# Gate and up products of a convolutional FFN by Strassen's rule, over two token halves, with the down product as a stage of its own

## The chip, the cores and the metric

The kernel runs on one core of a Trainium2 chip. The metric is the time of one execution on the device, in microseconds; of several runs the median. TensorE does the matrix products (PE in the profile; PEld is its loading of weights), VectorE (DVE) and ScalarE (ACT) and GpSimd (POOL) the element-wise work. Only VectorE and ScalarE read TensorE's results, which lie in eight PSUM banks of 512 fp32 columns; GpSimd works on SBUF alone. SyncE's queue (SP) issues loads, ScalarE's queue some stores.

## What is computed

One layer of a decoder for 1024 prompt tokens and 8 x 4 sample tokens, 1056 columns in all, in fp32: a combined projection, two token mixers, an output projection, and an FFN with a causal convolution of width 3 on the gate rows. The change touches what comes after the mixers:

```python
mix = jax.nn.sigmoid(gate_a) * y_a + jax.nn.sigmoid(gate_b) * y_b    # y_a, y_b: branch products
x = x + (mix @ w_out).astype(dt)                                     # w_out [1024, 1024]

h2 = _rmsnorm(x, g_ffn)
gc, new_ffn = _causal_conv(h2 @ w_ffn_gate, ffn_buf, w_ffn_conv)     # w_ffn_gate, w_ffn_up [1024, 2816]
x = x + ((jax.nn.silu(gc) * (h2 @ w_ffn_up)) @ w_ffn_down).astype(dt)  # w_ffn_down [2816, 1024]
# after the layer: y = _rmsnorm(x, g_final)
```

## The kernel before

Every operand of a large product is held as two rounded parts, hi and lo (`split`, line 82: a cast on ScalarE, line 83, and a subtraction on VectorE, line 84), and a product is three matmuls for each block of 128 input rows: hi x hi, hi x lo, lo x hi (`mm3`, lines 106 to 111). Activations lie in [channel, token] layout, eight blocks of 128 channels by 1056 tokens. `load_w` (line 86) fetches 256 weight columns in two loads of 512 KB on SP's queue and splits them; `proj_cm` (line 125) multiplies 128 of those columns with three blocks of 352 tokens, each in a PSUM bank of the pool `psd`, which has four.

After the mixers come the branch products (lines 1160 to 1179), blocks of 352 tokens; the output projection (lines 1195 to 1215), 256 columns at a time over nine token tiles, with residual, second norm (`norm`) and transposition to [channel, token] (`to_cm`); then the FFN. The 2816 features are 22 tiles of 128, taken two at a time in 11 chunks. `gate_up` does for each tile of a chunk three blocks for the gate, the convolution (`conv_proj`, one multiplication, line 229, and two fused steps, line 231, on VectorE; SiLU on ScalarE, line 232), then three blocks for up, each multiplied with the gate (line 1266) and split into `act` (lines 1268 and 1269). `down` (line 1276) multiplies the chunk's two tiles with 2 x 1024 down weights and adds the results to the residual `x1` in SBUF (line 1289; the sample rows line 1293). The loop emits `gate_up(ch + 1)` ahead of `down(ch)`, so that gate, up and down products alternate for the whole FFN, and `act` has two places. The last chunk's `down` ends each token tile with the final norm and its store.

The order in each engine's queue is not written by hand: the framework places an instruction when its inputs and buffers are ready, and prefers what stands earlier in the program.

Of the kernel before, what the change touches and what calls it, by code (L numbers as in the profile page):

```python
# [16 lines left out]
P = 128  # L17
# [16 lines left out]
OFF_Q, OFF_K, OFF_V, OFF_AB, OFF_OGA = 0, 512, 1024, 1536, 1544  # L34
OFF_QB, OFF_FB, OFF_IB, OFF_OGB, OFF_GA, OFF_GB = 2056, 2568, 3080, 3592, 4104, 5128
# [7 lines left out]
def hybrid_step(ctx: ExitStack, tc: tile.TileContext, ins, outs):  # L43
# [23 lines left out]
    # ---------------------------------------------------------------- constants  # L67
# [10 lines left out]
    # ---------------------------------------------------------------- helpers  # L78
# [6 lines left out]

    def load_w(parts, eng=None):
        """parts: list of halves; a half is a list of (row chunk count, DRAM AP [rows, 128 columns])."""
        hi = wpool.tile([P, KD, 256], F32R, name="whi")
        lo = wpool.tile([P, KD, 256], F32R, name="wlo")
        for j, half in enumerate(parts):  # L90
            raw = wpool.tile([P, KD, P], F32, name="wraw")
# [23 lines left out]
    def mm_s(ps, st, whi, wlo, ks):  # L115
        """The sample tokens' rows: st holds (hi | lo) columns; rows NS.. of ps take the low part's share."""
# [8 lines left out]
    def proj_cm(W, j, m, evac, src=None):  # L125
        """Generator: one block of BW tokens per step."""
# [10 lines left out]
    class Fill:  # L137
        """Dense work that is emitted between the steps of a token mixer."""
# [30 lines left out]
    def norm(t, xt, g_bc, work, xn, sq=None):  # L169
        """RMSNorm of token tile t (rows of xt), scaled by g_bc, into xn."""  # L170
# [8 lines left out]
    def to_cm(t, xn, dst):  # L179
        """Token tile t to [channel, token] layout, split into dst."""  # L180
# [14 lines left out]
    # ---------------------------------------------------------------- DRAM scratch  # L195
# [9 lines left out]
    def conv_proj(W, j, width, wT, cacheT, out_cache, dst, dst_s, zp, src=None):  # L205
        """Generator: project 128 channels, causal conv along tokens, SiLU; dst [P, SEQ], dst_s [P, NBAT * STEP]."""
# [26 lines left out]
        # the outputs of batch b start at column pad + SEQ + b * per of co  # L233
# [17 lines left out]
    # ---------------------------------------------------------------- first norm, first projections  # L251
    cwT = const.tile([P, 12, 28], F32, name="cwT")
    fwT = const.tile([P, NFF, 19], F32, name="fwT")
    lbT = const.tile([P, H, 2], F32, name="lbT")
    cout = const.tile([P, 12, 27], F32, name="cout")
    qkv_s = const.tile([P, 3, H, 32], F32, name="qkv_s")     # the sample tokens' columns stay on chip
# [14 lines left out]
    wab = ini.tile([P, KD, 16], F32R, name="wab")     # (hi | lo) of the decay and beta columns  # L271
# [95 lines left out]
    ab = const.tile([P, NT, 8], F32, name="ab")  # L367
# [12 lines left out]
    # ---------------------------------------------------------------- masks  # L380
    ones = const.tile([P, P], F32, name="ones")
    nc.gpsimd.memset(ones, 1.0)
    eem = const.tile([P, 2, P], F32, name="eem")      # (j<i | j<=i), rows j, columns i
# [4 lines left out]
    slow = const.tile([P, P], F32, name="slow")       # m > j  # L388
# [4 lines left out]
    bm = const.tile([P, NBLK, STEP], F32, name="bm")      # row and column belong to the same block  # L393
# [5 lines left out]
    m96 = const.tile([96, NBAT], F32, name="m96")         # a head's tokens and batches, three times  # L399
    for i in range(3):  # L400
        nc.gpsimd.tensor_copy(m96[32 * i:32 * i + 32, :], bm[32 * i:32 * i + 32, NBAT * i:NBAT * (i + 1), 0])
    eem_s = const.tile([P, 2, P], F32, name="eem_s")
    for k in range(2):
        nc.gpsimd.tensor_tensor(eem_s[:, k, :], eem[:, k, :], bmf, ALU.mult)
    slow_s = const.tile([P, P], F32, name="slow_s")
    nc.gpsimd.tensor_tensor(slow_s, slow, bmf, ALU.mult)
    last_s = const.tile([P, NBLK, STEP], F32, name="last_s")
# [931 lines left out]
```

## Time and profile before

| | |
|---|---|
| median of 3 runs | 1815.76 us (1807.79 to 1821.93) |
| span of the profiled execution | 1813.2 us |
| TensorE busy in it | 1766.7 us, 97% |
| VectorE / ScalarE / GpSimd busy | 52% / 28% / 10% |
| moved by DMA | 161.67 MB, mean 89 GB/s |
| branch products, out projection, FFN | from about 830, 930, 1035 us |

The times of instructions come from the profiled execution, which is one of its own; its span stands 2.6 us under the median of the runs. Matmuls overlap: a matmul's own duration is longer than the distance to the next, so the distance from start to start says what one costs.

### The profile page before, as it was taken

The page shows a single profiled execution, that of the slowest core. Times are in us where ns is not written, and L with a number is a line of the kernel's source. Part 1 is how long each engine was busy: PE and PEld are TensorE (multiplying, and loading weights), DVE is VectorE, ACT ScalarE, POOL GpSimd, SP SyncE. Part 2 cuts the span into 40 slices and gives each one's busy share as a digit, 9 for nine tenths or more (in the row PEclk, how much of TensorE's full clock was granted, in tenths as well). Part 3 has the DMA queues.
Part 4 walks back from the last instruction along what each step waited for, and adds up shares of the span by engine and source line. Part 5 has one row for each costly group of instructions (what it writes and reads, how often), then busy time and mean ns, then how long its engine had stood idle before and what let it go on. Part 6 is the DMA issues. An engine that isn't in the chain of part 4 may idle for free.

```text
span 1813.2 us, 28073 instructions
## 1 busy us (share of the span) xinstructions
PE 1766.7 (97%) x11591; PEld 1678.6 (93%) x11591; DVE 935.9 (52%) x1634; ACT 516.4 (28%) x1133; POOL 179.7 (10%) x332
## 2 busy tenths in 40 slices
PE   6999999999999999999999999999999999999998
PEld 6999898989899999999999999989989899899896
DVE  5555555756464657415542644453453454544456
ACT  5432525343332223323110432112112112122122
POOL 2200101111010234200000100000000000000001
PEclk9999999999998989999999999999999999999999
DMA  5233343453333434463433111111111111111102
GB/s 163 82 116 105 108 134 106 134 169 108 100 91 100 136 106 143 119 220 99 140 120 89 50 48 44 36 46 47 47 47 47 47 47 47 47 47 47 47 27 109
DMA packets 199947, 161.67 MB, mean 89 GB/s; under 512 B 17982, under 2 KB 186064, under 8 KB 199801
## 3 DMA queue, kind: packets, MB, share of 16 engines
q1 hardware_dynamic: 175382, 123.92, 23.5%
q10 hardware_dynamic: 24438, 35.96, 5.5%
q8 instruction: 91, 1.49, 0.3%
q14 instruction: 36, 0.29, 0.0%
HBM read 119.57 MB, written 40.21 MB: 88 GB/s over the span
## 4 chain that ended last, share of the span: by engine, by line
PE 78%; DVE 10%; DMA 3%; ACT 3%; issue 3%; POOL 1%; SPq 1%; ACTq 0%; POOLq 0%; DVEq 0%
PE pd L109 22%; PE pd L110 22%; PE pd L111 22%; DVE Pt L745 3%; PE pm L974 2%; DVE X L747 2%; DVE wlo L84 1%; DMA Db<-dU 1%; PE pd L121 1%; POOL rs L76 1%; DMA Yd<-dX 1%; DVE y L177 1%; POOL pss L76 1%; PE pm L606 0%; PE pm L829 0%
## 5 line engine op out<-in xcount | busy, mean ns | idle before, releaser
L109 PE MATMUL pd<-hhi,whi 128*128 128x352 f32 x1056 | 348.3, 330 | 0.4 <-ACT z L218 0.4
L111 PE MATMUL pd<-hhi,wlo 128*128 128x352 f32 x1056 | 346.3, 328 | 0.0
L110 PE MATMUL pd<-hlo,whi 128*128 128x352 f32 x1056 | 346.0, 328 | 0.0
L109 PE MATMUL pd<-mhi,whi 128*128 128x352 f32 x1056 | 340.5, 323 | 0.0
L110 PE MATMUL pd<-mlo,whi 128*128 128x352 f32 x1056 | 338.6, 321 | 0.7 <-DVE mlo L84 0.7
L111 PE MATMUL pd<-mhi,wlo 128*128 128x352 f32 x1056 | 338.3, 321 | 0.0
L84 DVE TENSOR_TENSOR wlo<-wraw,whi 128x1024 fp32r<-128x1024 f32 x130 | 157.6, 1223 | 204.7 <-ACT whi L83 204.2
L83 ACT CAST whi<-wraw 128x1024 fp32r<-128x1024 f32 x130 | 135.2, 1051 | 407.6 <-PE pd L111 202.0
L109 PEld LDWEIGHTS pd<-hhi,whi 128*128 128x128 f32 x1056 | 200.4, 190 | 1.9 <-ACT z L218 0.6
L110 PEld LDWEIGHTS pd<-hlo,whi 128*128 128x128 f32 x1056 | 200.7, 190 | 1.1 <-DVE hlo L84 0.4
L111 PEld LDWEIGHTS pd<-hhi,wlo 128*128 128x128 f32 x1056 | 200.3, 190 | 0.6
L110 PEld LDWEIGHTS pd<-mlo,whi 128*128 128x128 f32 x1056 | 198.4, 188 | 1.3 <-DVE mlo L84 0.9
L109 PEld LDWEIGHTS pd<-mhi,whi 128*128 128x128 f32 x1056 | 198.0, 188 | 0.4
L111 PEld LDWEIGHTS pd<-mhi,wlo 128*128 128x128 f32 x1056 | 198.0, 188 | 0.0
L1289 DVE TENSOR_TENSOR x<-x,pd 128x512 f32<-128x512 f32 x176 | 118.9, 686 | 78.0 <-PE pd L111 77.7
L109 PE MATMUL pd<-whi,act 128*128 128x512 f32 x352 | 138.0, 392 | 0.1
L110 PE MATMUL pd<-wlo,act 128*128 128x512 f32 x352 | 137.2, 390 | 0.0
L111 PE MATMUL pd<-whi,act 128*128 128x512 f32 x352 | 137.0, 389 | 0.0
L1266 DVE TENSOR_TENSOR ga<-pd,ga 128x352 f32<-128x352 f32 x66 | 34.5, 523 | 98.5 <-PE pd L111 98.5
L218 ACT COPY z<-pd 128x352 f32<-128x352 f32 (+1 forms) x102 | 44.1, 442 | 137.4 <-PE pd L111 129.4
L109 PEld LDWEIGHTS pd<-whi,act 128*128 128x128 f32 x352 | 66.1, 188 | 16.2 <-PE pd L111 2.0
L111 PEld LDWEIGHTS pd<-whi,act 128*128 128x128 f32 x352 | 66.1, 188 | 14.1
(411 smaller groups left out, 2760.5 us busy)
## 6 DMA issues: line engine op xcount, KB each, us to landing
wraw<-in_w_in SPq DMA_DIRECT2D x48, 512.0 KB
wraw<-in_w_ffn_gate SPq DMA_DIRECT2D x22, 512.0 KB
wraw<-in_w_ffn_up SPq DMA_DIRECT2D x22, 512.0 KB
wraw<-in_w_ffn_down SPq DMA_DIRECT2D x22, 512.0 KB
sg_d<-sg ACTq DMA_DIRECT2D x16, 528.0 KB
qkv_d<-sl ACTq DMA_DIRECT2D x12, 512.0 KB
sgb<-sg_d SPq DMA_DIRECT2D x12, 352.0 KB
sga<-sg_d SPq DMA_DIRECT2D x12, 352.0 KB
```

Source lines behind the costliest of these rows:

```text
L76: nc.gpsimd.tensor_tensor(out, in_, pexp[:n, which, :w], ALU.pow)
L83: nc.scalar.copy(out=hi, in_=src)
L84: (eng or nc.vector).tensor_tensor(lo, src, hi.bitcast(F32), ALU.subtract)
L109: nc.tensor.matmul(ps, whi[:, kw], xhi[:, kx], start=q == 0, stop=False)
L110: nc.tensor.matmul(ps, whi[:, kw], xlo[:, kx], start=False, stop=False)
L111: nc.tensor.matmul(ps, wlo[:, kw], xhi[:, kx], start=False, stop=q == n - 1)
L218: nc.scalar.copy(out=z[:, pad + a:pad + e], in_=ps[:, :e - a])
L745: nc.vector.tensor_tensor(Pt[:, :, 0:w], X[:, :, 0:w], Db[:, 0:w, r:w].rearrange("p s o -> p o s").broadcast_to([P, 8, w]), ALU.mult)
L747: nc.vector.tensor_reduce(X[:, :, r], Pt[:, :, 0:w], axis=mybir.AxisListType.X, op=ALU.add)
L974: nc.tensor.matmul(ps[:, cc * 64:(cc + 1) * 64].rearrange("p (n r) -> p n r", r=s), kk[:, cs], rhs, start=True, stop=True)
L1266: nc.vector.tensor_tensor(a[:, bs], ps, a[:, bs], ALU.mult)
L1289: nc.vector.tensor_tensor(x1[:, t, qs], x1[:, t, qs], ps, ALU.add)
```

## The change

Gate and up products: for two feature tiles and two token groups of equal width n (256 in the first half of the tokens, 272 in the second, which holds the sample tokens) the eight products of half the input channels become seven, by the Strassen-Winograd rule. `wino` computes them into four PSUM banks, three of which are used twice; ScalarE, VectorE and GpSimd combine them into the four blocks of the result. The weights' combinations are formed by GpSimd (`wino_weights`, once for each half), the activations' by VectorE and GpSimd (`wino_acts`, once for each half). The second half's operands are laid where the first half's lie. Weight buffers are a pool of five (`w8`) and four raw ones.

The result of the FFN's first part goes to DRAM (`act_d`), the residual too (`x1_d`). After all 44 calls the down product runs as a stage of its own: `load_act` fetches and splits a chunk's input, ahead of `down` of the chunk before; the first chunk writes its sums by ScalarE, the later ones add on VectorE; GpSimd adds the residual. The branch products go over four token blocks of 256 and 272 in place of three of 352. Constants of the mixers are freed after them.

```diff
-    for nb in range(NB):
+    for i, (b0, b1) in enumerate(QT):        # (0,256) (256,512) (512,784) (784,1056)
...
+    def wino_weights(w, f0):
+        r0, r1 = wraw(), wraw()
+        for r, f in ((r0, f0), (r1, f0 + 1)):
+            nc.sync.dma_start(out=r, in_=w[:, f * P:(f + 1) * P].rearrange("(k p) n -> p k n", p=P))
...
+        def group(src, n):
+            t = w8("wg").rearrange("p a b -> p (a b)").rearrange("p (s k n) -> p s k n", s=2, n=P)
+            split(t[:, 0, :n], t[:, 1, :n], src)
+            out.append(t)
+        a11, a12, a21, a22 = r0[:, :HK], r0[:, HK:], r1[:, :HK], r1[:, HK:]
...
+        yield out
+        s12 = pair_tile("s12")
+        nc.gpsimd.tensor_tensor(s12[:, HK:], a21, a22, ALU.add)
+        nc.gpsimd.tensor_tensor(s12[:, :HK], s12[:, HK:], a11, ALU.subtract)
+        group(r0, KD)
+        yield
+        s34 = pair_tile("s34")
+        nc.gpsimd.tensor_tensor(s34[:, :HK], a11, a21, ALU.subtract)
+        nc.gpsimd.tensor_tensor(s34[:, HK:], a12, s12[:, :HK], ALU.subtract)
+        group(s12, KD)
+        yield
+        group(s34, KD)
+        yield
+        group(a22, HK)
+        yield
...
+    def wino(W, X, n, gt, steps, c11, c12, c21, c22):
+        banks = [PSD(f"x{i}") for i in range(4)]
+        x1, x6, x5, x7 = (b[:, :n] for b in banks)
...
+            for k in range(HK):
+                w = W[g][:, :, k0 + k]
+                nc.tensor.matmul(ps, w[:, 0], hi[:, k], start=start and k == 0, stop=False, skip_group_check=True)
+                nc.tensor.matmul(ps, w[:, 0], lo[:, k], start=False, stop=False, skip_group_check=True)
+                nc.tensor.matmul(ps, w[:, 1], hi[:, k], start=False, stop=k == HK - 1, skip_group_check=True)
...
+        mm(0, x1, True)
+        m1 = tmp("m1")
+        nc.scalar.copy(out=m1, in_=x1)
+        mm(1, x6, True)
+        u2 = tmp("u2")
+        nc.vector.tensor_tensor(u2, m1, x6, ALU.add)
+        next(steps, None)
+        mm(2, x5, True)
+        m5 = tmp("m5")
+        nc.scalar.copy(out=m5, in_=x5)
+        mm(3, x7, True)
+        u3 = tmp("u3")
+        nc.vector.tensor_tensor(u3, u2, x7, ALU.add)
+        c22(u3, m5)
+        mm(4, x1, False)
+        c11(x1)
+        next(steps, None)
+        mm(5, x5, False)
+        c12(u2, x5)
+        next(steps, None)
+        mm(6, x7, False)
+        c21(u2, x7)
+        next(steps, None)
...
+    def wino_acts(src, n, tb, ops):
...
+        split(*ops[0], b11)
+        nc.vector.tensor_tensor(t1, b12, b11, ALU.subtract)
+        nc.vector.tensor_tensor(t2, b22, t1, ALU.subtract)
+        yield
+        split(*ops[1], t2)
+        nc.gpsimd.tensor_tensor(b12, b22, b12, ALU.subtract)
+        yield
+        split(*ops[2], t1)
+        nc.gpsimd.tensor_tensor(t4, b21, t2, ALU.subtract)
...
+    def gate(f0, half, X, W, steps, ga, z):
...
+        wino(W, X, n, gt, steps,
+             lambda x: nc.scalar.copy(out=z[:, 0, 2:2 + n], in_=x),
+             lambda u, x: q2(0, lambda o, c, t: nc.vector.tensor_tensor(o, cut(u, c, t), cut(x, c, t), ALU.add)),
+             lambda u, x: nc.vector.tensor_tensor(z[:, 1, 2:2 + n], u, x, ALU.add),
+             lambda u, m: q2(1, lambda o, c, t: nc.gpsimd.tensor_tensor(o, cut(u, c, t), cut(m, c, t), ALU.add)))
...
+            nc.scalar.activation(co[:, f, :cw], z[:, f, 0:cw], AF.Copy, scale=wT[:, 0:1])
+            for q in (1, 2):
+                nc.vector.scalar_tensor_tensor(co[:, f, :cw], z[:, f, q:q + cw], wT[:, q:q + 1], co[:, f, :cw],
+                                               ALU.mult, ALU.add)
+        nc.scalar.activation(ga[:, :, :MID], co[:, :, :MID], AF.Silu)
...
+    def up(f0, half, X, W, steps, ga, a):
...
+             lambda u, m: nc.gpsimd.tensor_tensor(a[:, 1, n:w], u, m, ALU.add))
+        nc.vector.tensor_tensor(a[:, 0, n:w], a[:, 0, n:w], ga[:, 0, n:w], ALU.mult)
+        nc.vector.tensor_tensor(a[:, 1, :w], a[:, 1, :w], ga[:, 1, :w], ALU.mult)
+        nc.scalar.dma_start(out=act_d[f0:f0 + 2, :, t0:t0 + w].rearrange("f p t -> p f t"), in_=a[:, :, :w])
+    todo = [(half, f0, k) for half in range(2) for f0 in range(0, NFF, 2) for k in range(2)]
...
+    def load_act(ch):
         s0 = 2 * (ch % 2)
...
+        r = fp.tile([P, 2, T], F32, name="ra")
+        nc.sync.dma_start(out=r, in_=act_d[2 * ch:2 * ch + 2].rearrange("f p t -> p f t"))
+        nc.scalar.copy(out=ahi[:, s0:s0 + 2, :T], in_=r)
+        hv = ahi[:, s0:s0 + 2].bitcast(F32)
+        nc.vector.tensor_tensor(alo[:, s0:s0 + 2, :SEQ], r[:, :, :SEQ], hv[:, :, :SEQ], ALU.subtract)
+        nc.vector.tensor_tensor(ahi[:, s0:s0 + 2, T:], r[:, :, SEQ:], hv[:, :, SEQ:T], ALU.subtract)
...
+    nc.sync.dma_start(out=x1s, in_=x1_d[SEQ:, :])
+    x1r = post.tile([P, KD, 2 * 2 * QW], F32, name="x1r", tag="mA")
+    nc.sync.dma_start(out=x1r[:, :, :D], in_=x1_d[:SEQ, :].rearrange("(t p) d -> p t d", p=P))
...
+    Wd = load_down(0)
+    load_act(0)
     for ch in range(NCH):
         if ch + 1 < NCH:
-            gate_up(ch + 1)
+            Wn = load_down(2 * ch + 2)
+            load_act(ch + 1)
...
+        down(ch, *Wd)
+        Wd = Wn
```

## Rows read from the trace of the kernel before

**Rows 1.** The page's head: span, busy time and share of each engine, granted clock.

```profile
span 1813.2 us, 28073 instructions
PE 1766.7 (97%) x11591; PEld 1678.6 (93%) x11591; DVE 935.9 (52%) x1634; ACT 516.4 (28%) x1133; POOL 179.7 (10%) x332
...
PEclk9999999999998989999999999999999999999999
```

**Rows 2.** Table by stage: stretch, length, busy time of each engine (instructions), clock, DMA, GB/s.

```profile
830.00:932.00 102.00, 99.57 (x624) 98.90 (x624) 66.14 (x99) 28.64 (x41) 0.00 (x0) 0.98 0.46 134
...
1029.00:1050.00 21.00, 18.74 (x127) 17.80 (x126) 13.85 (x22) 10.55 (x22) 3.23 (x7) 1.00 0.18 51
1050.00:1758.00 708.00, 707.88 (x4040) 662.70 (x4039) 329.70 (x459) 148.22 (x261) 27.59 (x85) 1.00 0.15 45
```

**Rows 3.** Timeline of TensorE, gate and up: start, duration in us; first and last of 26.

```profile
1299.72 0.32 PE L110 MATMUL pd<-mlo,whi 128*128 128x352 f32 x1
...
1303.68 0.32 PE L111 MATMUL pd<-mhi,wlo 128*128 128x352 f32 x1
```

**Rows 4.** The same in the output projection: first and last of 21.

```profile
984.58 0.28 PE L111 MATMUL pd<-whi,mlo 128*128 128x256 f32 x1
...
986.96 0.28 PE L110 MATMUL pd<-wlo,mhi 128*128 128x256 f32 x1
```

**Rows 5.** The same in the down product: first and last of 10.

```profile
1769.78 0.39 PE L110 MATMUL pd<-wlo,act 128*128 128x512 f32 x1
...
1771.82 0.39 PE L110 MATMUL pd<-wlo,act 128*128 128x512 f32 x1
```

**Rows 6.** Groups of VectorE by shape: count, busy us, mean ns, idle time before and releaser.

```profile
L84 DVE TENSOR_TENSOR wlo<-wraw,whi 128x1024 fp32r<-128x1024 f32 x130 | 157.6, 1223 | 204.7 <-ACT whi L83 204.2
L1289 DVE TENSOR_TENSOR x<-x,pd 128x512 f32<-128x512 f32 x176 | 118.9, 686 | 78.0 <-PE pd L111 77.7
...
L1293 DVE TENSOR_TENSOR x1s<-x1s,pd 32x512 f32<-32x512 f32 x44 | 28.2, 672 | 1.1 <-PE pd L123 0.7
...
L1207 DVE TENSOR_TENSOR x<-res,pd 128x256 f32<-128x256 f32 x32 | 13.4, 419 | 48.3 <-PE pd L111 48.2
L720 DVE SCALAR_TENSOR_TENSOR UA<-pm,pr,EE 128x256 f32<-128x256 f32 x32 | 13.2, 474 | 0.0
...
L84 DVE TENSOR_TENSOR mlo<-pm,mhi 128x512 fp32r<-128x512 f32 x16 | 10.5, 680 | 0.0
...
L177 DVE SCALAR_TENSOR_TENSOR tmp<-x,rs,tmp 128x1024 f32<-128x1024 f32 x8 | 10.3, 1285 | 5.6 <-POOL rs L76 5.6
```

**Rows 7.** The same for ScalarE.

```profile
L83 ACT CAST whi<-wraw 128x1024 fp32r<-128x1024 f32 x130 | 135.2, 1051 | 407.6 <-PE pd L111 202.0 <-PE pd L110 133.3 <-PE pd L123 66.2
```

**Rows 8.** The same for GpSimd.

```profile
L989 POOL TENSOR_TENSOR kk<-kk,tots 128x256 f32<-128x256 f32 x48 | 35.1, 734 | 34.3 <-issue 13.2 <-PE pm L974 11.3 <-PE pm L962 4.3
...
L658 POOL TENSOR_TENSOR Sb<-Sb,eGl_s 128x512 f32<-128x512 f32 x8 | 8.3, 1040 | 73.1 <-DMA Sb<-in_state_delta 63.7 <-DMA Db<-dU 9.3
```

**Rows 9.** Line 654 (min/median/max ns), and timeline of VectorE and GpSimd at 701 us.

```profile
L654 DVE TENSOR_TENSOR um<-st,m x16: 676/679/1479, 316.6 to 738.8; 96x512 fp32r<-96x512 f32 x16
...
701.33 1.48 DVE L654 TENSOR_TENSOR um<-st,m 96x512 fp32r<-96x512 f32 x1
...
701.22 1.04 POOL L658 TENSOR_TENSOR Sb<-Sb,tots_s 128x512 f32<-128x512 f32 x1 [3.34 <-DMA Sb<-in_state_hgrn]
```

**Rows 10.** Timeline of VectorE in the FFN.

```profile
1108.88 1.32 DVE L231 SCALAR_TENSOR_TENSOR co<-z,fwT,co 128x1072 f32<-128x1072 f32 x1
1110.12 0.51 DVE L1266 TENSOR_TENSOR ga<-pd,ga 128x352 f32<-128x352 f32 x1
1110.56 1.32 DVE L231 SCALAR_TENSOR_TENSOR co<-z,fwT,co 128x1072 f32<-128x1072 f32 x1
```

**Rows 11.** Timeline of SP's queue at the largest load, and two us of it by stage.

```profile
772.52 1.52 SPq L1146 DMA_DIRECT2D raw<-oT_d  x3
...
778.00:780.00 2.00, 2.00 (x14) 2.00 (x13) 0.00 (x0) 0.00 (x0) 0.00 (x0) 1.00 1.01 408
```

**Rows 12.** Table by stage: the ten us around TensorE's gap at 830 us.

```profile
830.00:840.00 10.00, 7.92 (x39) 7.54 (x39) 7.95 (x14) 9.97 (x19) 0.00 (x0) 0.83 0.47 143
```

More of the change, by code (lines that the diff above doesn't have):

```diff
@@ new lines, in to_raw @@
+    def to_raw(t):
+        n = rows(t)
+        dst, c0 = (hA, t * P) if t * P < MID else (hB, t * P - MID)
+        for g in range(2):
+            ps = PSM()
+            pv = ps.rearrange("p (k n) -> p k n", k=4)
+            for k in range(4):
+                nc.tensor.transpose(out=pv[:, k, :n], in_=x1t(t)[:n, (4 * g + k) * P:(4 * g + k + 1) * P],
+                                    identity=ident[:n, :n])
+            nc.scalar.copy(out=dst[:, 4 * g:4 * g + 4, c0:c0 + n], in_=pv[:, :, :n])
@@ L1195, in hybrid_step, with first_weights @@
+    def first_weights():
+        g = wino_weights(wg, 0)
+        return next(g), g
     for q in range(4):
@@ L1225, in hybrid_step @@
-    last = {}
+                norm2(t)
+                if 3 <= t < 7:
+                    to_raw(t - 3)
+                if t in (4, 5):
+                    next(gen_n)
+                if t == 6:
+                    o1 = post.tile([P, 2, KD, 2 * QW], F32R, name="o1", tag="mA")
+                    o1 = o1.rearrange("p a k t -> p (a k t)").rearrange("p (i s k t) -> p i s k t", i=4, s=2, k=HK)
+                    opsA = [(o1[:, i, 0, :, :256], o1[:, i, 1, :, :256]) for i in range(4)]
+                    opsA += [None] * 3
+                    genA = wino_acts(hA, 256, hT[:, KD * MID:], opsA)
+                    for _ in range(2):
+                        next(genA)
@@ new lines, in hybrid_step, with fetch, mixed, mixedB @@
+    todo = [(half, f0, k) for half in range(2) for f0 in range(0, NFF, 2) for k in range(2)]
+    for _ in gen_n:
+        pass
+    queue = []
+    def fetch(i):
+        if i < len(todo):
+            g = wino_weights((wg, wu)[todo[i][2]], todo[i][1])
+            queue.append((next(g), g))
+    fetch(1)
+    W = Wn
+    late = []
+    for i, (half, f0, k) in enumerate(todo):
+        fetch(i + 2)
+        Wnext, gn = queue.pop(0) if queue else (None, iter(()))
+        if i == 0:
+            def mixed(gn):
+                for _ in genA:
+                    pass
+                next(gn)
+                to_raw(4)
+                yield
+                to_raw(5)
+                next(gn)
+                yield
+                to_raw(6)
+                next(gn)
+                yield
+                to_raw(7)
+                to_raw(8)
+                next(gn)
+                yield
+            gn = mixed(gn)
+        elif half == 0 and i == NCH * 2 - 1:
+            genB = wino_acts(hB, QW, hT[:, :KD * MID], opsB)
+            def mixedB(gn):
+                next(gn)
+                yield
+                next(genB)
+                next(genB)
+                next(gn)
+                yield
+                next(genB)
+                next(gn)
+                yield
+                next(genB)
+                next(gn)
+                yield
+            gn = mixedB(gn)
+        X = opsA if half == 0 else opsB
+        n2 = (i // 2) % 2
+        if k == 0:
+            gate(f0, half, X, W, gn, gab[n2], zb[n2])
+        else:
+            up(f0, half, X, W, gn, gab[n2], ab_[n2])
+        if half == 0 and i == NCH * 2 - 1:
+            for _ in genB:
+                pass
+        W = Wnext
```

298 lines of the change are left out of this document (189 added, 109 removed).

## The prediction

> **What bounds the kernel now.** I read the head of the page first: TensorE is busy for 97% of the span and holds the full clock in nearly every slice, VectorE is busy 52%, GpSimd 10% [rows 1]. A busy TensorE is not yet a saturated one, so the second view is the table by stage: from 1050 to 1758 us, where the FFN runs, TensorE has no idle time at all, VectorE is busy 47% and GpSimd 4%; in the branch and out projections before it the gaps are a few us [rows 2]. The third view is the stream of matmuls itself, for the distance from start to start. A 352-column matmul starts every 158.4 ns (25 distances from 1299.72 to 1303.68 us) [rows 3], a 256-column one every 119.0 ns (20 distances from 984.58 to 986.96) [rows 4], a 512-column one every 226.7 ns (9 from 1769.78 to 1771.82) [rows 5]. So the FFN is bound by TensorE's columns: 0.41 ns a column between 256 and 352, and some 14 ns that each matmul costs whatever its width. What the other engines do there is hidden, and may grow until it isn't.
>
> **What the change removes.** A pair of feature tiles takes 288 matmuls of 352 columns for gate and up, 11 pairs take 3168: 3168 x 0.1584 = 501.8 us. After, one call of the 7-product routine is 7 x 4 x 3 = 84 matmuls, 256 wide in the first token half and 272 in the second, and there are 22 calls for each half: 1848 x 0.1190 + 1848 x 0.1256 = 452.0 us (0.1256 by the slope above) [rows 3, 4]. That is 49.8 us less. 7/8 of the work would be 62.7 us less; the rest goes on more and narrower matmuls.
>
> **What it adds, in order of the program.**
>
> *Branch products.* Three blocks of 352 become four of 256 and 272: 576 x 0.1584 = 91.2 us become 384 x 0.1190 + 384 x 0.1256 = 93.9, so +2.7.
>
> *The calls themselves.* Two calls (gate, up) are TensorE's 168 x 0.1190 = 20.0 us, in the second half 21.1. Under them must now go, twice as often as before since weights are fetched and split for each half: six splits of 1024 elements and two of 512, the eight weight sums on GpSimd, nine product combinations of 256 from PSUM, four convolution steps of 512, two multiplications. VectorE alone by the rows: 6 x 1.22 + 2 x 0.68 + 9 x 0.42 + 4 x 0.74 (between 0.47 at 256 and 1.29 at 1024) + 1.1 = 16.5 us [rows 6]. ScalarE: 6 x 1.05 for the casts and some 5 for copies and SiLU, 11 us [rows 7]. GpSimd: 8 x 1.04 + 2 x 0.73 = 9.8 us [rows 8]. Each fits under 20. But GpSimd and VectorE get in each other's way: at 701.33 a VectorE multiplication of 512 elements whose inputs both lie in SBUF took 1.48 us, where its median is 0.68; a GpSimd instruction had started at 701.22, and VectorE's ends 0.55 us after it [rows 9]. One waited for the other, and only 0.13 us of its own start was hidden. VectorE's instructions of that kind are the splits, the convolution steps and the multiplications, 16.5 - 9 x 0.42 = 12.7 us; with GpSimd's 9.8 that is 22.5 us for what can't overlap, less 0.13 for each of 24 instructions, 19.4 us out of 20.0. So the shared resource is nearly full, and VectorE must in addition do its 3.8 us of PSUM work, which can overlap. Bounds: 0 if the waits fall into VectorE's idle 3.5 us; if everything on VectorE and GpSimd is serial, 16.5 + 9.8 - 3.1 = 23.2, so 3 us a pair of calls. I take 0.7, nearer the lower end, because the row at 1108.88 shows that the queues aren't filled in the order written (an up product is placed between two convolution steps of the gate [rows 10]), so an instruction that is ready goes into a hole; 22 pairs make +15 (0 to 66). The same reordering is why I don't add up the chain that the written order would make (SiLU on ScalarE ahead of the next call's first copy).
>
> The Trainium skill, page "SBUF — State Buffer", section "Who interferes with whom", says that a VectorE instruction with two SBUF inputs and a GpSimd instruction that reads SBUF exclude each other for the whole instruction. The trace agrees on who waits, and shows that a little of the start is hidden (0.55 instead of 0.68 us) [rows 9]. With whole instructions the sum would be 22.5 us a pair, 2.5 us over TensorE's 20.0, or 55 us in all instead of my 15.
>
> *Entering the FFN.* Seven operand splits and two sums are 9 x 1.22 = 11 us on VectorE, among the last three norms; the first call can start on the first operand. Today this stretch has TensorE idle 2.3 of 21 us [rows 2]. +3 (0 to 10).
>
> *Between the halves.* The operands of the second half take the place of the first half's, which the last call still reads: again nine steps, 1088 wide, about 11.6 us, against the 3.5 to 5 us that VectorE has free in a pair. +6 (2 to 12).
>
> *Entering the down stage.* Today the down product alternates with gate and up, and its input never leaves the chip. After, the input goes through DRAM and the first chunk waits for it. Ahead of it on SP's queue stands the residual, 4.19 MB, whose load waits for a buffer that the last call's fourth product frees, 4.5 us before TensorE's last product ends. The only load of that size in the trace (three transfers issued at 772.52) moved at up to 408 GB/s [rows 11]: 10.2 us, plus 1.08 MB of input, 2.6 us, plus a cast of 2112 elements, 2.1 us, and a split of as many, 2.4 us [rows 6, 7]. -4.5 + 1.5 for the start of a transfer + 10.2 + 2.6 + 2.1 + 2.6 = 14.5 us from TensorE's last product; 22 transposes of the convolution cache fall into it. The clock: in the ten us at 830, with about 2 us idle, the granted clock was 0.83, which is a third of the window at 1.2 instead of 2.4 GHz, 1.7 us lost [rows 12]. +15 (6 if the input goes ahead of the residual; 22 at half that rate).
>
> *The down stage.* TensorE's work is the same, 104 matmuls of 512 a chunk, 23.6 us. VectorE has 16 x 0.69 + 4 x 0.67 for the sums and 5 us for the next chunk's splits, 18.7: it fits on average. But next chunk's operands go into what the chunk before has just left: so at each change of chunk the two weight splits (2.4), and the input's split (2.1 behind a cast, 2.4 itself), 5.5 us together, stand ahead of the first evacuation on VectorE, and TensorE's fifth group waits for that. With four PSUM banks TensorE goes on for four groups, 2 x 0.9 + 2 x 1.36 = 4.5 us; the first bank comes free after the two sums of the sample rows, at 6.8. So 2.2 us of waiting, at nine changes: +20 (0 to 25; 0 if the sums are placed ahead of the splits).
>
> **Hidden.** Weights twice (23 MB more), input and residual out and in (33 MB): the DMA share in the FFN is 0.15 today [rows 2], and 1 MB a call is 100 GB/s. The conv's first multiplication goes from VectorE to ScalarE, which has room. ScalarE's queue gets 22 stores of the FFN's input and 9 of the residual, some 0.35 us of issue each; the 22 wait for the up product's last multiplication, and behind each stands the next call's first copy, which TensorE needs only at its fifth product, 5.7 us on.
>
> **Sum.** 1813.2 - 49.8 + 2.7 + 15 + 3 + 6 + 15 + 20 = 1825 us against the profiled span of 1813.2 [rows 1]; that span lies 2.6 us under the median of the runs shown, 1815.8, so I say 1828.
>
> **Rivals.**
> Faster: the waits between VectorE and GpSimd fall into idle time and the down stage's evacuations go ahead of the splits. For it: every engine has room on average, and the reordering of [rows 10]. Against: four banks are just one call's, and a split once begun isn't interrupted. 1813.2 - 49.8 + 2.7 + 24 = 1790, 1793 with the offset. It decides below some 0.3 us lost a pair of calls.
> Slower: VectorE and GpSimd run one after the other, 3 us a pair over TensorE: 1825 + 51 = 1876, 1879. For it: the full stop in [rows 9]. Against: only 11 of some 34 instructions of a pair are GpSimd's. It is slower by over 1% from 1 us a pair on. The rule of the page named above gives 1865.
> The entry into the down stage is worse than I have it (the residual at half the rate, and the second chunk's load behind it too): another 10 to 20 us, 1840 to 1848.
> That narrow matmuls don't get cheaper, so that the change does not do what it says: excluded by the 119.0 ns of [rows 4], which hold for this kernel's own operands and weight loads. That the doubled weight transfers bind: 5 us a call at half the rate of [rows 11], against 10; hardly.
>
> **How the numbers follow.** My forecast about 0.34, the faster rival 0.28, the slower one 0.27, the worse entry 0.07, the rest 0.04. About 1% (18 us) is what a measurement of this kernel can tell from no change; my forecast lies within it, the faster rival 1.3% under, the slower 3.4% over. Of the forecast's own spread (1808 to 1845) a part is over 1834. So faster 0.31, same 0.31, slower 0.38. The range, 1785 to 1880, reaches from just under the faster rival to the slower; the forecast's own is 1808 to 1845.
>
> **What would show it.** Right: matmuls of 256 and 272 columns every 119 and 126 ns in long runs; two calls at 20.5 to 21 us; VectorE's splits often at about 2 us instead of 1.22, ended by GpSimd; one gap of 10 to 15 us at the change to the down stage, ended by the input's cast and split; nine gaps of about 2 us in it, each ended by VectorE's x1s sum. Wrong: pairs at 20.0 or above 23, no gaps at the changes of chunk, or a gap of over 25 us ahead of the down stage.

## The result, and the profile after

The changed kernel takes 1911.78 us, the kernel before 1814.72 in the same comparison (medians of four runs each); the ratio estimated from the runs is 1.0524, with an interval of 1.0489 to 1.0558. The forecast was 1828, its range ended at 1880. The profiled execution of the changed kernel has a span of 1909.7 us, 96.5 more than [rows 1].

The head of its page:

```profile
span 1909.7 us, 30870 instructions
PE 1751.6 (92%) x12311; PEld 1650.5 (86%) x12311; DVE 1273.5 (67%) x1921; ACT 681.7 (36%) x1314; POOL 582.7 (31%) x575
...
DVE  5555555756556574055426899999999991666666
...
PEclk9999999999999899999999899998999997999999
```

TensorE is busy 15 us less than in [rows 1], in a span that is 96.5 longer. VectorE's line stands at 9 over ten slices, which are gate and up. The table by stage of the changed kernel (stretch, length, busy time of each engine, clock, DMA share, GB/s), against [rows 2]:

```profile
1016.00:1079.00 63.00, 49.10 (x345) 46.98 (x345) 47.95 (x50) 35.49 (x57) 42.50 (x33) 0.84 0.27 88
1079.00:1305.00 226.00, 207.77 (x1669) 204.39 (x1668) 220.95 (x229) 111.60 (x160) 170.59 (x120) 0.97 0.38 117
...
1334.00:1570.00 236.00, 218.17 (x1707) 215.53 (x1707) 231.55 (x248) 118.95 (x185) 187.38 (x165) 1.00 0.38 118
1570.00:1600.00 30.00, 4.20 (x29) 2.61 (x28) 5.41 (x7) 7.17 (x10) 0.00 (x0) 0.62 0.80 292
1600.00:1855.00 255.00, 229.34 (x955) 180.13 (x954) 158.09 (x206) 43.90 (x42) 20.06 (x8) 0.95 0.20 67
```

In both halves (second and third line) VectorE is busy 98% and TensorE 92%: the bound has changed engines. What TensorE waited for after 1016 us (total in us, times, longest):

```profile
PE x L1260 <- DVE u L1279: 39.2, 28, 3.5
PE pd L119 <- DVE x1s L1596: 25.7, 9, 5.3
PE pd L130 <- DVE act L1577: 24.9, 1, 24.9
PE x L1261 <- DVE o L88: 6.2, 5, 2.6
PE x L1260 <- ACT m L1276: 5.7, 3, 4.1
```

The first line is the start of the seventh product, which needs a bank that VectorE's sum `u3` must have read. The time by stages in us, from the start of the first matmul of each to the start of its last:

| | before | after |
|---|---|---|
| branch products | 94.5 | 104.3 |
| gate and up | 501.8 by its matmuls | 538.4 (452.0 by its matmuls) |
| last up product to first down product | - | 28.7 |
| down product | 259.3 by its matmuls | 299.0 |
| FFN in all | 772.5 | 866.1 |
| last matmul to the end | 8.9 | 11.8 |

The FFN's +93.6, the branch's +9.8 and the end's +2.9, less 3.2 in the out projection and behind it and less 6.7 before the branch, make up the 96.5, but for rounding. The stages before the branch are the same work in both; over the kernels below the FFN's first matmul lies anywhere from 1020 to 1040 us, so spans of single executions are compared by their stages.

Gate and up lie 86.4 us over their matmuls, of which a pair of calls (gate and up of two feature tiles) has 20.0 us in the first half of the tokens and 21.1 in the second. The first pair of calls takes 47.2 us (27.2 over), ten pairs of the first half 22.56 in the median (28.8 over in all), the change of halves two pairs of 30.9 and 25.4 (14.1 over), the steady pairs of the second half 23.11 (16.1 over).

### The profile page after: what moved, and what is told of

It reads as the page before. It is cut to its first block, busy times and chain, and to the rows that moved or that the text cites. A ratio compares the mean times of both kernels' runs of the same rounds, so it can differ in the third digit from the quotient of the medians.

```text
span 1909.7 us, 30870 instructions
## 1 busy us (share of the span) xinstructions
PE 1751.6 (92%) x12311; PEld 1650.5 (86%) x12311; DVE 1273.5 (67%) x1921; ACT 681.7 (36%) x1314; POOL 582.7 (31%) x575
## 5 line engine op out<-in xcount | busy, mean ns | idle before, releaser
L1260 PE MATMUL x<-o,wg 128*128 128x256 f32 (+1 forms) x1232 | 361.9, 294 | 48.3 <-DVE u L1279 39.2
L1261 PE MATMUL x<-o,wg 128*128 128x256 f32 (+1 forms) x1232 | 358.3, 291 | 6.2 <-DVE o L88 6.2
L1262 PE MATMUL x<-o,wg 128*128 128x256 f32 (+1 forms) x1232 | 358.0, 291 | 0.6 <-DVE wg L88 0.6
L1260 PEld LDWEIGHTS x<-o,wg 128*128 128x128 f32 x1232 | 239.5, 195 | 55.4 <-DVE u L1279 45.0
L1261 PEld LDWEIGHTS x<-o,wg 128*128 128x128 f32 x1232 | 239.5, 194 | 7.5 <-DVE o L88 7.5
L1262 PEld LDWEIGHTS x<-o,wg 128*128 128x128 f32 x1232 | 239.7, 195 | 0.8 <-DVE wg L88 0.8
L88 DVE TENSOR_TENSOR wlo<-wraw,whi 128x1024 fp32r<-128x1024 f32 x86 | 105.2, 1233 | 118.5 <-issue 59.2
L119 PE MATMUL pd<-whi,act 128*128 128x512 f32 x352 | 142.4, 404 | 25.8 <-DVE x1s L1596 25.7
L1590 DVE TENSOR_TENSOR acc<-acc,pd 128x512 f32<-128x512 f32 x160 | 108.2, 686 | 81.1 <-PE pd L121 80.6
L80 POOL TENSOR_TENSOR rs<-ss,pexp 128x1 f32<-128x1 f32 (+1 forms) x27 | 14.8, 549 | 445.3 <-DVE ss L185 443.0
L88 DVE TENSOR_TENSOR wg<-s,wg 128x1024 fp32r<-128x1024 f32 x88 | 138.3, 1572 | 8.2 <-ACT wg L87 7.2
L121 PE MATMUL pd<-whi,act 128*128 128x512 f32 x352 | 140.1, 398 | 0.0
L88 DVE TENSOR_TENSOR wg<-wraw,wg 128x1024 fp32r<-128x1024 f32 x88 | 134.3, 1526 | 0.0
L119 PEld LDWEIGHTS pd<-whi,act 128*128 128x128 f32 x352 | 68.6, 195 | 44.9 <-issue 29.7
L1463 DVE SCALAR_TENSOR_TENSOR F<-F,fwT 128x512 f32<-128x512 f32 (+1 forms) x88 | 104.1, 1238 | 0.4 <-ACT F L1461 0.4
```

The source lines that it names most:

```text
L88: (eng or nc.vector).tensor_tensor(lo, src, hi.bitcast(F32), ALU.subtract)
L119: nc.tensor.matmul(ps, whi[:, kw], xhi[:, kx], start=q == 0, stop=False)
L121: nc.tensor.matmul(ps, wlo[:, kw], xhi[:, kx], start=False, stop=q == n - 1)
L1260: nc.tensor.matmul(ps, w[:, 0], hi[:, k], start=start and k == 0, stop=False, skip_group_check=True)
L1261: nc.tensor.matmul(ps, w[:, 0], lo[:, k], start=False, stop=False, skip_group_check=True)
L1262: nc.tensor.matmul(ps, w[:, 1], hi[:, k], start=False, stop=k == HK - 1, skip_group_check=True)
```

## The experiments

Theory A: a VectorE instruction with two SBUF operands and a GpSimd instruction shut each other out, and GpSimd's weight sums take from VectorE the time that it lacks. Its rivals: B, the sums are a slow link ahead of the splits, which come late for that reason; C, VectorE has too much work of its own, sums or not. For the gap ahead of the down stage, the input's load waits either for memory that small stores still hold, or for the data's own way out and back. For the nine gaps inside that stage, either the splits hold the first sums up because they stand in one block, or each split is too long by itself.

The first eight kernels were run once each, so they are read by their stages; the last five ran four to twelve times.

**Without the sums.**

```diff
-        group(s12, KD)
+        group(r1, KD)
...
-        group(s34, KD)
+        group(r0, KD)
```

with the four `nc.gpsimd.tensor_tensor` on `s12` and `s34` taken out. The kernel leaves the sums out, so its gate and up products are not the layer's.

> Leaves out the four GpSimd sums of each weight pair: the splits read the raw weights in their place (same shapes), so the gate and up products are not the reference's. Theory A (VectorE's two-operand instructions and GpSimd's sums exclude each other, and VectorE at 98% is what holds the pairs of calls): the weight splits fall from a mean of 1.55-1.6 us to 1.22-1.3, a steady pair of calls from 22.56 to 20.0-20.7 us in the first half and from 23.11 to 21.1-21.8 in the second, the entry to the FFN gets 8-15 us shorter, the whole 1848-1862 us. Theory B (the sums are a link in the chain load - sum - cast - split, and the operands are late because the link is slow): the same fall here. Theory C (VectorE and ScalarE are too slow by their own work, sums or not): pairs stay above 22 us, the whole above 1895.

The span is 1825.6 us, 23 under the lower end of what was expected; half of that is that the FFN began 11 us earlier in this execution. Gate and up take 466.4 us, that is 72.0 less; pairs take 19.88 and 21.19, which is the matmuls alone, and the first pair 32.9. C falls. VectorE's groups by shape (mean ns of one), of the changed kernel and of this one:

```profile
L88 DVE TENSOR_TENSOR wg<-s,wg 128x1024 fp32r<-128x1024 f32 x69 | 109.0, 1579 | 7.0 <-ACT wg L87 6.4
L88 DVE TENSOR_TENSOR wg<-wraw,wg 128x1024 fp32r<-128x1024 f32 x34 | 71.9, 2115 | 0.0
L1463 DVE SCALAR_TENSOR_TENSOR F<-F,fwT 128x512 f32<-128x512 f32 x40 | 44.0, 1157 | 0.0
```

```profile
L88 DVE TENSOR_TENSOR wg<-wraw,wg 128x1024 fp32r<-128x1024 f32 x116 | 142.4, 1228 | 88.2 <-ACT wg L87 87.1
L1457 DVE SCALAR_TENSOR_TENSOR F<-F,fwT 128x512 f32<-128x512 f32 x36 | 24.6, 746 | 0.0
```

The same split costs 1.23 us alone and 1.58 to 2.12 beside the sums. VectorE is not slowed as a whole: its sums `u2`, with one input in PSUM, take the same time in both kernels (the changed one first; min/median/max in ns), which is what A says of two SBUF operands:

```profile
L1272 DVE TENSOR_TENSOR u<-m,x x44: 406/422/431, 1057.8 to 1564.6; 128x256 f32<-128x256 f32 x22, 128x272 f32<-128x272 f32 x22
```

```profile
L1266 DVE TENSOR_TENSOR u<-m,x x44: 407/422/439, 1034.5 to 1481.1; 128x256 f32<-128x256 f32 x22, 128x272 f32<-128x272 f32 x22
```

**The sums made, but read by nobody.** As above, with the four sums left in.

> The four GpSimd sums still run on the same weights, but nobody reads them: the splits read the raw weights, so the gate and up products are not the reference's. Theory A (the sums cost VectorE its port time whoever waits for them): pairs stay at 22.2-22.8 and 22.8-23.3 us, splits stay near 1.55 us, the whole 1895-1912 us. Theory B (the sums are late as a link of the chain): pairs fall to 20.0-20.7 and 21.1-21.8 as without sums, the whole 1848-1865 us.

The span is 1921.5 us, gate and up 550.7, pairs 23.28 and 24.22. B falls too: no split reads a sum, and the loss is all back. The groups of VectorE and GpSimd in this run, and a stretch of its first half:

```profile
L88 DVE TENSOR_TENSOR wg<-wraw,wg 128x1024 fp32r<-128x1024 f32 x100 | 166.9, 1670 | 13.0 <-ACT wg L87 13.0
...
L1237 POOL TENSOR_TENSOR s<-wraw 128x512 f32<-128x512 f32 x33 | 70.5, 2138 | 0.0
...
1100.00:1240.00 140.00, 123.35 (x1015) 120.71 (x1015) 124.23 (x139) 66.50 (x96) 108.54 (x73) 1.00 0.38 114
```

It is 12 us above the changed kernel, and the pairs lie above what was expected; why the unread sums cost that much more stays open. VectorE is busy 89% here and not 98%, and the weight loads wait longer for the splits to free the raw buffers (340 us in all from 1080 to 1480, 140 in the changed kernel). So this run shows that the sums cost time though nobody reads them, but not that a full VectorE is the only way in which they do.

**The sums on VectorE**: `nc.gpsimd` becomes `nc.vector` in four lines.

> The four weight sums run on VectorE in place of GpSimd. Theory (a 512-column sum costs VectorE some 0.68 us of its own but takes 1.3 us from it as an exclusion when GpSimd does it): VectorE gets 5.4 us more work in a pair of calls, and without sums it was idle for some 4.4 us of one ahead of its splits, so a pair takes 20.3-21.3 us in the first half and 21.3-22.0 in the second, the first pair 33-42, the whole 1860-1885 us. Rival (the element work of the two engines together is too much wherever it runs): pairs stay at 22.3 us and more, the whole over 1900 us.

The span is 1853.1 us, gate and up 483.7, 54.7 less. Pairs take 20.1 and 21.19 us, a little under what was expected, as is the whole; the first takes 35.8. A stretch of the first half, and the sum's row:

```profile
1100.00:1240.00 140.00, 137.07 (x1138) 136.31 (x1137) 139.80 (x213) 76.01 (x109) 33.59 (x27) 0.99 0.42 128
...
L1232 DVE TENSOR_TENSOR s<-wraw 128x512 f32<-128x512 f32 x14 | 9.5, 679 | 0.0
```

VectorE is busy for 139.8 of 140 us and yet TensorE for 98%: eight sums of 0.68 us on the busier engine are cheaper than eight on the idle one.

**The second half loads the sums that the first half stored.**

```diff
+        nc.scalar.dma_start(out=sd[0], in_=s12)     # first half; s34 likewise
...
+        nc.sync.dma_start(out=s34, in_=sd[1])       # second half; s12 likewise
```

> The first half stores its two tiles of weight sums to memory (1 MB in each call), the second half loads them and forms none. Theory: the first half stays at 22.4-22.9 us a pair, the second falls from 23.11 to 21.2-21.5, the change of halves gets 2-6 us shorter, the whole 1883-1895 us. Rival (the loads take the place of the sums: the sum tiles have two buffers, so a tile is loaded only when the one before it is split): the second half stays above 22.5 us a pair, the whole 1900-1915 us.

The span is 1884.5 us. The second half is 21.19 a pair, as expected, and the change of halves falls to 22.8 and 21.2; the first half rises to 24.22, which was not. ScalarE's timeline there (start, duration, [idle before, releaser]):

```profile
1206.19 0.33 ACTq L1255 DMA_DIRECT2D ws_d<-s  x1
1206.62 1.34 ACT L1478 ACTIVATE F<-F,fwT 128x512 f32<-128x512 f32 x2 [4.18 <-POOL s L1248]
1207.86 0.35 ACT L1286 COPY m<-x 128x256 f32<-128x256 f32 x1
```

The store's issue waits on ScalarE's queue for GpSimd's sum, and the copy out of TensorE's bank (line 1286) stands behind it.

**Eight products in the same frame**: `blocks` in place of `wino`, four results of 24 matmuls each, evacuated straight from PSUM; no sums of weights, tokens or products.

> Undoes Strassen's rule alone: two token halves, the block order, the stored activations and the separate down stage stay, but each call makes eight block products (96 matmuls of 256 or 272 columns in place of 84) and needs no sums of weights, tokens or products. Theory (the seven products cost as much in stalls as they save in matmuls): TensorE streams without a stall, a pair of calls takes 22.8-23.0 us in the first half and 24.1-24.3 in the second, the first pair under 30, the gate and up stage 520-530 us against 538, the whole 1893-1908 us. Rival (the seven products still win something, the loss lies in the separate down stage): gate and up over 545 us, the whole over 1915 us.

The span is 1895.3 us, gate and up 520.4 without a stall. With its sums on GpSimd the seven-product form loses 18 us to the eight; what its matmuls save is more than eaten.

**The residual's load later**; in the second kernel also **memory of its own for the convolution cache** (its sums `fout` and its transposed rows `rowt` lie no more where the input's buffers will).

```diff
+    nc.scalar.copy(out=x1r[:, 0, :8], in_=ahi[:, 0, :8].bitcast(F32))   # makes the load wait
     nc.sync.dma_start(out=x1r[:, :, :D], in_=x1_d[:SEQ, :].rearrange("(t p) d -> p t d", p=P))
...
-    fout = fp.tile([P, NFF, 18], F32, name="fout")
+    fout = room(6 * ZW + 4 * HB, NFF * 18).rearrange("p (f t) -> p f t", t=18)
```

> Only the 4 MB load of the residual is moved: it starts once the first activation chunk of the down product has been cast (a copy of 8 columns into its target makes it wait), and its sums go to chunks 2 to 5 in place of 1 to 4. Theory (the small stores of the convolution cache stood behind this load, the activation load waited for their memory): the gap ahead of the down product falls from 25.2 us to 11-15 us, the stores land in about 2 us each, the whole 1898-1903 us. Rival (the activation's store, load, cast and split set the gap by themselves): it stays at 22-26 us, the whole 1907-1914 us.

> As the run with the late residual, and besides the convolution cache's sums and its transposed rows get memory that the down stage's input buffers don't share. Theory (what was left of the gap, 19.5 us, is the activation load waiting for memory that the cache's small stores hold): the load starts when the activation's own store has landed, the gap falls to 9-12 us and the whole lies 7-11 us below the late residual run once the stages before the FFN are set equal. Rival (the stores of the last activation and the down weights' loads set it): the gap stays at 17-20 us.

From the last up product to the first down product it is 28.7 us in the changed kernel, 23.0 with the late load, 16.2 with memory too (TensorE idle for 24.9, 19.3 and 12.4). Both gain, both less than expected. ScalarE's timeline of the changed kernel at the place, and SP's:

```profile
1573.91 0.32 ACTq L259 DMA_DIRECT2D out<-rowt  x1
1582.56 0.57 ACT L257 COPY rowt<-pm 18x512 f32<-18x512 f32 x1 [9.22 <-DMA out<-rowt]
...
1588.78 0.57 ACT L257 COPY rowt<-pm 18x512 f32<-18x512 f32 x1 [4.31 <-DMA out<-rowt]
...
1594.24 1.95 ACT L1574 CAST act<-ra 128x2112 fp32r<-128x2112 f32 x1 [2.34 <-DMA ra<-act_d]
```

```profile
1565.88 0.38 SPq L1611 DMA_DIRECT2D x1r<-x_d  x1
1582.43 1.75 SPq L1566 DMA_DIRECT2D wraw<-in_w_ffn_down  x4
1589.20 9.88 SPq L1573 DMA_DIRECT2D ra<-act_d  x3
...
SPq L1566 <- DMA x1r<-x_d: 16.0, 1, 16.0
SPq L1573 <- DMA out<-rowt: 10.0, 3, 4.9
```

The residual's load goes out at 1565.88. Then SP's queue stands for 16.0 us, a wait that the profile puts down to this load's landing (last lines: SP's own waits from 1540 to 1600). Meanwhile small stores of the cache take 9.2 us to free their tile, and later 4.3. The input's load, whose buffer lies where those tiles lie, goes out at 1589.20, released by such a store. With the late load the small stores are faster but not fast, against the 2 us that were expected:

```profile
1573.19 0.57 ACT L257 COPY rowt<-pm 18x512 f32<-18x512 f32 x1 [4.86 <-DMA out<-rowt]
```

What slows them there, with no residual in flight, was not tried; on the same queue the last call's store of its result stands ahead of them.

**The down product's splits spread over the chunk before**: the generator `chunk` is stepped after the first, third and fifth row tile of `down`.

```diff
+            if 0 < t < 7 and t % 2:
+                next(steps, None)
```

> Only the place of the down product's operand splits changes: the next chunk's three VectorE splits (2 x 1.2 and 2.3 us) are emitted after the first, third and fifth row tile of the running chunk, and not in one block at its end. Theory (the block of 4.7 us and more on VectorE keeps the first banks of a chunk from coming free): the nine gaps of 2.5-3.0 us, 28.8 us in all, fall to under 0.6 us each; the down stage goes from 299 to 270-275 us, the whole 1883-1890 us. Rival (each split is itself longer than the slack of the four banks, so the stall is only cut into three pieces): the down stage stays at 290-300 us, the whole 1903-1914 us.

The span is 1869.0 us. The down stage falls from 299.0 to 262.5 us, 36.5 less and more than was expected; the nine gaps held 27.1 (29.2 from start to start, less nine matmuls of 0.227). The block in the changed kernel, on VectorE's timeline:

```profile
1625.36 2.36 DVE L88 TENSOR_TENSOR wlo<-wraw,whi 128x1024 fp32r<-128x1024 f32 x2 [18.64 <-PE pd L120]
1627.64 2.29 DVE L1576 TENSOR_TENSOR act<-ra,act 128x2048 fp32r<-128x2048 f32 x1
1629.84 0.22 DVE L1577 TENSOR_TENSOR act<-ra,act 128x64 fp32r<-128x64 f32 x1
1630.09 2.58 DVE L1596 TENSOR_TENSOR x1s<-x1s,pd 32x512 f32<-32x512 f32 x4
```

and TensorE's waits inside the stage with the splits spread:

```profile
PE pd L119 <- DVE acc L1596: 0.3, 1, 0.3
PE pd L119 <- DVE x1s L1602: 0.2, 1, 0.2
```

The other 9.4 us are nearly all the clock's, in the last section.

One of the nine gaps is 5.7 us where the others are 2.5 to 3.0. There VectorE's split of the input, 2.29 us above, ran beside GpSimd's sum of the residual, 2.39 or 2.40 us the seven other times, and both took longer, as theory A has it (timelines of GpSimd and VectorE):

```profile
1736.48 3.29 POOL L1598 TENSOR_TENSOR acc<-acc,x1r 128x1024 f32<-128x1024 f32 x1 [1.76 <-DVE acc L1590]
...
1737.45 4.46 DVE L1576 TENSOR_TENSOR act<-ra,act 128x2048 fp32r<-128x2048 f32 x1
```

**The repairs together, with seven and with eight products.** VectorE's sums, spread splits, late residual, own memory; the eight products with the last three.

> Three repairs together on the seven products: weight sums on VectorE, the down product's splits spread over the running chunk, and the late residual with the cache's own memory. If the three losses are separate they add up: 1853 us of the run with sums on VectorE, less 36 of the spread splits, less 12 of the gap, 1805, so 1795-1815 us, a pair of calls 20.0-20.3 and 21.2 us, the gap 11-14 us, the down stage 261-266 us. Rival (what one repair frees is lost again in another stage, as when the late residual's load meets the spread splits' loads): over 1822 us.

> The eight block products in the same repaired frame (spread splits, late residual, own memory). Theory (with its sums out of the exclusion Strassen's rule earns what its matmuls promise, less the entry and the change of halves): gate and up stay at 519-523 us where the seven take 480-487, and the whole is 1840-1855 us, 35-45 above the seven. Rival (the seven's gain is eaten elsewhere): less than 15 us between the two.

The seven take 0.9993 of the kernel before (0.9967 to 1.0020): gate and up 484.2 us, to the down product 14.8, down 262.2. The eight take 1.0107 (1.0058 to 1.0157): 520.4, 1.8, 261.0. The three losses add up. In gate and up the seven win 36 us over the eight; in the whole they win 25 by the medians and not the 35 to 45 expected, because with eight products the gap ahead of the down product is gone. The input's loads (first and last start) in the changed kernel and with eight:

```profile
L1573 SPq DMA_DIRECT2D ra<-act_d x11: 360/377/378, 1589.2 to 1798.4; - x11
```

```profile
L1514 SPq DMA_DIRECT2D ra<-act_d x11: 366/377/462, 1503.6 to 1741.0; - x11
```

The first chunk's input is features 0 to 255, which have been in memory since the second half's first pair. With eight products there are no temporaries `m1`, `u2`, `m5`, `u3`, in whose memory the load's buffer lies, and it goes out some 55 us before the last product.

**GpSimd's sums of token operands on VectorE too.**

> As the repaired seven, and GpSimd's two sums of token operands (128x1024 each, made at the entry to the FFN and at the change of halves) go to VectorE too. Theory (they still shut VectorE out there: one of its normalizations took 3.39 us in place of 1.28): the first pair of calls falls from 35.8 to 29-33 us, the change of halves from 30.7 to 25-29, the whole 4-10 us below the repaired seven. Rival (VectorE is the limit of both places by its own queue): the two places stay within 2 us, the whole within 3 us.

The time is 0.9966 of the kernel before (0.9940 to 0.9992), by the medians 2.9 us below the seven, where 4 to 10 were expected. The first pair falls from 35.3 to 32.6 as expected; the change of halves does not (31.4 against 30.5), which there leaves the rival, VectorE's own queue. Gate and up take 480.0 us.

**The first input in other memory**, then **a tile for each row group of the cache** and the residual behind the second chunk's input.

```diff
+            rs = [gp.tile([P, T], F32, name="ra0", tag="sl").rearrange("p (o t) -> p o t", o=1) for _ in range(2)]
```

> As the repaired seven with the operand sums on VectorE; besides, the down product's first input goes into two scratch tiles that are free a call earlier, in place of a buffer that shares memory with the last call's temporaries. The data itself has lain in memory since the second half's first pair; with eight products, which have no such temporaries, the gap was 1.6 us. Theory (what is left of the gap, 11-13 us, is that memory and not the data's way through memory): the load goes out before the last call ends, the gap falls to 1-4 us, the whole 8-12 us below the run before, a ratio of 0.987-0.992 to the kernel before. Rival (the input's cast and split behind the last call's own work on ScalarE and VectorE keep it): the gap stays at 8 us or more, the ratio at 0.994-0.999.

> As the run with the early first input; besides, the convolution cache's transposed rows get a tile each (four of 512 columns, three of 256 in the temporaries), so that ScalarE waits for no small store, and the residual's load waits for the second chunk's input in place of the first's (its sums go to chunks 3 to 6). Theory (the 10.9 us stall that came in place of the gap is ScalarE held by a tile whose store lay behind the residual's load, ahead of the first evacuations): no stall over 2 us in the first 40 us of the down stage, the stage at 261-265 us in place of 274, the ratio to the kernel before 0.984-0.992. Rival (the first chunks wait for their own loads, whatever holds the rows): a stall of 6 us or more stays, the ratio 0.993-0.999.

With the first alone the gap falls to 1.6 us, so it was that memory, and a stall of 10.9 us comes up in the first chunk: 0.9973 (0.9944 to 1.0002), nothing won. TensorE's wait and ScalarE's timeline:

```profile
PE pd L119 <- ACT acc L1607: 10.5, 1, 10.5
...
1526.70 0.84 ACT L257 COPY rowt<-pm 18x512 f32<-18x512 f32 x2 [9.19 <-DMA out<-rowt]
...
1531.25 2.05 ACT L1607 COPY acc<-pd 128x512 f32<-128x512 f32 x4 [3.71 <-DMA out<-rowt]
```

The residual's load now goes out at 1508.72, the cache's stores take up to 9.2 us while it is in flight, and ScalarE holds the first evacuations behind them. With the second edit:

```profile
PE pd L119 <- ACT acc L1611: 4.1, 1, 4.1
```

The stall falls to 4.5 us, over the 2 expected and under the rival's 6, the stage falls from 273.9 to 266.4, and the whole to 1796.74 us, a ratio of 0.9895 (0.9855 to 0.9934) to the kernel before. It is the one version that is faster by about 1%. The stage came in just over the expected 261 to 265. The edit changes two things, the tiles and the place of the residual's load; which of them counted was not tried, nor what holds the last 4.5 us.

## Why the prediction was wrong

*Right.* The matmuls: 118 and 126 ns, and 19.88 and 21.19 us for a pair without the sums, against 20.0 and 21.1. The signs that it named appeared: splits at about 2 us, a gap ended by the input's cast and split, nine gaps ended by the `x1s` sums. So did two of its signs of being wrong: pairs above 23 us (23.11 in the second half), and ahead of the down stage 28.7 us with TensorE idle for 24.9. Each term of the sum exists; nearly every one was too small:

| step | predicted, us | measured, us |
|---|---|---|
| VectorE and GpSimd, steady pairs | 15 | 44.9 (28.8 + 16.1) |
| entering the FFN | 3 | 27.2 |
| between the halves | 6 | 14.1 |
| entering the down stage | 15 | 28.7 |
| the down stage | 20 | 39.7 (299.0 - 259.3) |
| branch products | 2.7 | 9.8 |
| end | 0 | 2.9 |

The terms' excess is 105.6 us; 11.4 of it the FFN before had already spent beyond its matmuls (772.5 - 501.8 - 259.3, half of it on 47 transposes), which the sum had kept, and 9.9 came back ahead of the FFN.

*The step that failed first* is the 0.7 us a pair for the mutual waits of VectorE and GpSimd. The mechanism was right, and "serial at 3 us a pair" stood there as a rival; measured are 2.6 and 2.0. Two things were off. GpSimd's sum was priced at 1.04 us from [rows 8], from a product that reads one operand repeated along its row; with two full operands it takes up to 1.28 us here where VectorE is idle:

```profile
1051.10 1.28 POOL L1233 TENSOR_TENSOR s<-s,wraw 128x512 f32<-128x512 f32 x1
1052.34 1.27 POOL L1237 TENSOR_TENSOR s<-wraw 128x512 f32<-128x512 f32 x1
```

With that the prediction's own working gives 12.7 + 8 x 1.28 + 2 x 0.73 - 24 x 0.13 = 21.3 us in place of 19.4, which is over TensorE's 20.0 already. And it let VectorE's 3.8 us on PSUM overlap entirely: by an estimate from the same working, 22.56 - 21.3, about a third of it did not. The Trainium skill, page "GPSIMD Engine Reference", section "4.1 Engine selection", would have priced the sum higher: it puts GpSimd at about twice VectorE's time for two-input work; 1.28 against VectorE's 0.68 us in the run with the sums there agrees. The lower end was chosen by [rows 10], that ready instructions fill holes; at 98% VectorE has no hole. The rule that the prediction quotes from the Trainium skill (page "SBUF — State Buffer", section "Who interferes with whom") says the right thing about who shuts out whom; its 22.5 us a pair meets the 22.56 by the low price of the sum, with 1.28 it would be 24.4.

*The same cause in two other steps.* Entering the FFN and the change of halves were priced from VectorE's own instruction times. Without the weight sums the first pair falls by 14.3 of its 27.2 us and the two pairs of the change by 12.5 of their 14.1. So 72 us of the changed kernel's time hang on GpSimd's sums and the resource that they share with VectorE, and three terms that the prediction drew separately were wrong together. That is why the range, which reached to one rival at a time, did not hold.

*Entering the down stage.* The prediction made its 14.5 us out of the data's way: residual ahead in the queue, input, cast, split. Behind the issue of the input's load it was nearly right, 9.6 us (1589.20 to 1598.8) against 8.8 (1.5 + 2.6 + 2.1 + 2.6). What failed is the time ahead of the issue, 19.1 us from TensorE's last product against 5.7 (10.2 - 4.5). The residual's load went out about when it was expected, 4.2 us before the last product, but SP's queue stood for 16.0 us behind it and not for 10.2; half the rate, which the prediction named as its upper case, comes by its own terms to 25 or more and not to 22. The rest was no part of the prediction: the input, in memory for over 200 us, had no buffer, because the memory was first the cache's rows', with their slow small stores, and then the last call's temporaries'. So taking the residual away won only 5.7 us, and the two kinds of memory the rest.

*The down stage.* The block of splits ahead of the sums was right, at 27.1 us for nine gaps in place of 20. Its 5.5 us for the block is 0.7 over its own two parts of 2.4, and the block took 4.7 (1625.36 to 1630.06); but the sums of both halves of the sample rows alternate, so the first bank is free only after the third sum (in that gap it ends at 1632.07, and TensorE starts again at 1632.22), not after the second. Of the rest of the 39.7 nearly all is the clock, which the prediction put at nothing inside this stage.

*The branch products* and the 3 us at the end were not taken apart: the first have a gap of 4.0 us and smaller ones, which stay in the repaired versions.

## What to carry to other kernels

Before giving an idle engine element work, check what it shuts out. Time on GpSimd was here also taken from VectorE where the latter reads two SBUF operands, so add the two up as one resource over the busiest stretch, and price every term that uses it from that sum. Ask of a load not only when its data is ready but what its buffer's memory was before, and whose stores still read it. When a removed wait moves, look next at in-order queues: a copy that waits for a small store holds every evacuation behind it.

## What the hardware showed beside this

Short gaps cost more than their length. In the down stage of the changed kernel 61 of the 1144 matmuls start more than 0.3 us (and under 1 us) after the one before, where 0.227 is the median; 55 of them stand behind the long gap ahead of the stage and behind five of the nine, and all cost 25.7 - 61 x 0.227 = 11.9 us. Behind the gap of 5.7 us at 1738 the granted clock is 0.65, partly the lower level of 1.2 GHz; after the long one it is 0.50:

```profile
1598.00:1602.00 4.00, 3.21 (x8) 1.60 (x9) 0.85 (x3) 1.95 (x1) 0.00 (x0) 0.50 0.78 271
...
1744.00:1750.00 6.00, 5.91 (x18) 4.71 (x19) 3.22 (x5) 0.00 (x0) 0.00 (x0) 0.65 0.41 167
1750.00:1756.00 6.00, 6.00 (x28) 4.99 (x27) 2.92 (x5) 0.00 (x0) 0.00 (x0) 1.00 0.00 0
```

With the splits spread 12 such matmuls are left, 2.6 us. So nine gaps of 27.1 us were worth 36.5.

Gate and up have such matmuls too: 175 of the 3696 start 0.19 to 0.27 us after the one before, about twice the usual distance, and 17 of the 86.4 us over the matmuls lie in them. Whether they lengthened that stage, or only filled time in which VectorE was the limit anyway, is not shown.
